# A last product's last K pair by column halves, and two swapped load buffers

## The chip, the cores and the metric

The kernel runs on one core of a Trainium2 chip. The metric is the device time of one execution in microseconds (us). TensorE (PE in the profile) multiplies; VectorE (DVE), ScalarE (ACT) and GpSimd (POOL) work on tiles; SyncE (SP) issues most DMAs. Matrix products are summed in PSUM, which the other engines read from; everything else is held in SBUF.

## What is computed

One Conformer-like encoder layer on 256 tokens of width 2048, in float32: two half-weighted SwiGLU feed-forwards with 5632 hidden features, between them a mixing layer and a cross-attention into 256 memory tokens, and a final RMS norm. What matters here is the end:

```python
def swiglu_ffn(h, w_in, w_out):
    gate, up = jnp.split(h @ w_in, 2, axis=-1)
    return (jax.nn.silu(gate) * up) @ w_out
...
    h = rms_norm(x, ffn2_norm[l])
    x = x + MACARON_SCALE * swiglu_ffn(h, ffn2_w_in[l], ffn2_w_out[l])
return rms_norm(x, final_norm)
```

## The kernel before

**Products in two parts.** Every float32 operand is split into a rounded part and its remainder (`hi` and `lo`; ACT rounds, DVE subtracts), and a product is three matmuls: hi by hi, hi by lo, lo by hi. The split weights lie in tiles `hl`, of which there are a few in turn.

**The second feed-forward, first product.** `FeedForward.run` goes through the 5632 hidden features in eleven groups j of 512 (gate and up together 1024 columns), and within a group through 16 K tiles k of 128 features. Some pairs of K tiles are done in a form with seven products in place of eight (`seven`), the others plainly (`eight`). For a few plain tiles the split isn't made by DVE: the raw tile is loaded, ACT writes the rounded part and the negated raw tile (L426, L427), and POOL issues a DMA that loads the weights a second time and adds them onto the negated copy (L428). These are the "summed" tiles. In the second feed-forward (`pair=True`) they are K tiles 2, 7 and 13 of groups 1 to 7 and K tiles 2 and 10 of groups 8 to 10, 27 in all, listed in order in `sums_at`. The code of such a tile is `summed`.

They live in two buffers for the split tile, `hls[0]` (a tile of its own, `hl_s`) and `hls[1]` (`hl_s2`), with a raw buffer each: `raws_summed[0]` is a part of `spare`, `raws_summed[1]` is the place of hidden group 8, `h8`. From group 8 on the second pair is given up: group 8's result is written to `h8`, and `hl_s2`'s place is taken by groups 9 and 10. `buffer(at)` (L411) says which buffer an entry of the list has; `following(at)` finds the next entry with the same buffer. When `eight` has issued the matmuls of a summed tile, it notes the following entry, and that entry's load and copies are issued behind the next cast of the ordinary stream. Entry 0 is issued in group 0 at K tile 13, entry 1 behind group 0.

**The last product.** The hidden features are turned (transposed through TensorE) into tiles `hA`, `hB`, `hC`, and multiplied by `ffn2_w_out` in four blocks of 512 output columns. For the fourth block (L1276 and below) the two blocks of 128 tokens are set apart, so that the first can be finished while the second is multiplied: the 44 K tiles go in 22 pairs; all pairs are multiplied for token block 0 in order, and for token block 1 too, but for the last four pairs, whose split weights are kept (the first of these four in a tile `held`) and multiplied for block 1 at the end. `acc[0]` and `acc[1]` are one PSUM bank each (128 partitions by 512 columns). `by_token` issues the six matmuls of a pair.

**The end of a token block.** `add_up` adds half the product onto the residual `x2` (DVE, L1227), squares it with a running sum into a column of `sums` (ACT, L1231), and multiplies by the final gain (POOL, L1232). The sums of the first three blocks are gathered earlier into `most`, one value a token. `give` takes the root of the whole sum (L1238 to L1242), scales the row and stores it, in 2 parts for token block 0 and in 4 for block 1; the last part is scaled by ACT (L1248), the others by DVE (L1251).

**Order.** The order of each engine's instructions is made by a planner, which takes those whose operands are ready by its own reckoning and prefers what is written first; `tc.issue_after` holds it to an order in some places. Semaphores between engines are put in by the same tool. Small tiles of the pool `st` lie ahead of most larger pools; two fillers of 32 bytes, `to_64` and `to_64_too`, are among them.

Of the kernel before, what the change touches and what calls it, by code (L numbers as in the profile page):

```python
# [11 lines left out]
F32 = mybir.dt.float32  # L12
F32R = mybir.dt.float32r
AF = mybir.ActivationFunctionType
ALU = mybir.AluOpType
AX = mybir.AxisListType

P = 128
D = 2048
# [59 lines left out]
def layer(ctx: ExitStack, tc: tile.TileContext, a: dict):  # L79
    nc = tc.nc  # L80
    out = a["out"]
# [6 lines left out]
    st = ctx.enter_context(tc.tile_pool(name="st", bufs=1))  # L88
# [85 lines left out]
    def gemm_t(w, x_hl, per=0.0, acc=None, ks=None, joint=False, between=None):  # L174

        return ahead([w], x_hl, per, [acc], ks, joint, between=between)[0]
# [59 lines left out]
    def col(name, k):  # L236
        return pv[:, PV[name][0] + k:PV[name][0] + k + 1]
# [104 lines left out]
    class FeedForward:  # L342
# [67 lines left out]

        def buffer(self, at):  # L411

            return at % 2 if not self.pair or self.sums_at[at][0] < 8 else 0

        def following(self, at):
            same = [i for i in range(at + 1, len(self.sums_at)) if self.buffer(i) == self.buffer(at)]
# [384 lines left out]
    with ExitStack() as stack:  # L801
        with tc.tile_pool(name="mix", bufs=1) as pool:
# [78 lines left out]
            for n in range(NCT // 2):  # L881
                if n < 2:
                    acc = gemm_n(a["w_mix_vg"][n], lambda k: x_hl[:, k], per=1.35, between=turns, acc=accs[n], ks=range(8, KD, 2))
                else:
                    load_gate(n)
                    later.appendleft((1.6, memory_parts(n)))
                    acc = gemm_n(a["w_mix_vg"][n], lambda k: x_hl[:, k], per=1.35, between=turns, after=2)
# [3 lines left out]
                for t in range(2):  # L891
# [3 lines left out]
                        out=o[:, t], in0=acc[t][:, :T], scalar=r_t[:, t:t + 1], in1=tg, op0=ALU.mult, op1=ALU.mult  # L895
# [48 lines left out]
            for n in range(2):  # L944
                acc = gemm_n(a["w_mix_v"][n], lambda k: x_hl[:, k], per=1.35, between=turns)
                for t in range(2):
                    nc.scalar.activation(
                        out=vs[:, t, n * 512:(n + 1) * 512], in_=acc[t], func=AF.Gelu, scale=r_t[:, t:t + 1]
# [60 lines left out]
            for n in range(HEADS):  # L1009
                acc = gemm_n(a["w_k"][n], lambda k: m_hl[:, k], per=1.35, between=turns)  # L1010
# [16 lines left out]
            for n in range(2):  # L1027
                acc = gemm_n(a["w_mix_u"][n], lambda k: x_hl[:, k], per=1.35, between=turns)
# [13 lines left out]
            at = [part for _, part in later].index(conv_swish_0)  # L1042
# [10 lines left out]
            for h in range(HEADS):  # L1053
                acc = gemm_n(a["w_v"][h], lambda k: m_hl[:, k], per=1.6)
                for t in range(2):
                    nc.scalar.activation(
                        out=vv[:, t, h * HD:(h + 1) * HD], in_=acc[t], func=AF.Copy, scale=r_mt[:, t:t + 1]
# [8 lines left out]
            for f in range(KD):  # L1066
                if f < 3:
                    acc = gemm_t(a["w_mix_out"][f], lambda k: y_hl[:, k], acc=accs[f], ks=[(0, 8)])
                else:
                    acc = gemm_t(a["w_mix_out"][f], lambda k: y_hl[:, k])  # L1070
# [3 lines left out]
        with tc.tile_pool(name="attn", bufs=1) as pool:  # L1074
# [112 lines left out]
            for f in range(KD):  # L1187
                if f < 4:
                    acc = gemm_t(a["w_o"][f], o_of, acc=accs[f], ks=[(12, 4)] if f < 3 else [(8, 8)])
                else:  # L1190
                    acc = gemm_t(a["w_o"][f], o_of)
# [3 lines left out]
    with ExitStack() as stack:  # L1195
        ff = FeedForward(stack, ("S0", "S1", "S2"), x_hl, lambda k: col("ffn2_norm", k), a["ffn2_w_in"], PATTERNS[1], SUMMED[1], pair=True)
        x2 = ff.x2

        def turn(n, i, j):

            def go():
                q = j % 4
                dst = x2[32 * q:32 * q + 32, j // 4, n * 512:(n + 1) * 512].rearrange("p (f n) -> p f n", n=P)
                nc.vector.transpose(
                    out=dst[:, :, 32 * i:32 * i + 32],
                    in_=xT[32 * i:32 * i + 32, 4 * n:4 * n + 4, 32 * j:32 * j + 32],
                )
            return go

        h = ff.of  # L1210
        def first_beside(k):
            if k in (6, 9, 12):
                ff.sides(k // 3 - 2)

        turns = ff.run(lambda k: None, first_beside, lambda: rms_cols(ss, D, "r_x2"))
        put(0.3, *[turn(0, i, j) for i in range(4) for j in range(8)])
        acc_0 = gemm_n(a["ffn2_w_out"][0], h, per=0.55, between=turns, after=0)
        finish()
        ff.high.close()
        stack.enter_context(ff.late)  # L1220
        late = stack.enter_context(tc.tile_pool(name="late", bufs=1, reuse_waits="tile"))
        gf = late.tile([P, D], F32, name="gf")
        nc.sync.dma_start(out=gf, in_=a["final_norm"].partition_broadcast(P))
        sums = st.tile([P, 2, 4], F32, name="sums")

        def add_up(t, s, acc, i):
            nc.vector.scalar_tensor_tensor(  # L1227
                out=x2[:, t, s], in0=acc, scalar=0.5, in1=x2[:, t, s], op0=ALU.mult, op1=ALU.add
            )
            sq = late.tile([P, 512], F32, name="sq2")  # L1230
            nc.scalar.activation(out=sq, in_=x2[:, t, s], func=AF.Square, accum_out=sums[:, t, i:i + 1])  # L1231
            nc.gpsimd.tensor_tensor(out=x2[:, t, s], in0=x2[:, t, s], in1=gf[:, s], op=ALU.mult)  # L1232

        def give(t, parts):

            v, s, r = [st.tile([P, 1], F32, name=f"{n}{t}") for n in ("f_v", "f_s", "f_r")]
            last = sums[:, t, 3:4]
            nc.scalar.activation(out=s, in_=last, func=AF.Sqrt, scale=1.0 / D, bias=most[t])  # L1238
            nc.vector.tensor_scalar(out=v, in0=last, scalar1=1.0 / D, scalar2=most[t], op0=ALU.mult, op1=ALU.add)
            nc.vector.reciprocal(out=r, in_=s)  # L1240
            nc.vector.tensor_scalar(out=r, in0=v, scalar1=r, scalar2=s, op0=ALU.mult, op1=ALU.add)
            nc.vector.reciprocal(out=r, in_=r)  # L1242
            for i, (at, size) in enumerate(cuts(D, D // parts)):
                c = slice(at, at + size)
                if i == parts - 1:
                    r2 = st.tile([P, 1], F32, name=f"f_r2{t}")
                    nc.scalar.mul(out=r2, in_=r, mul=2.0)
                    nc.scalar.activation(out=x2[:, t, c], in_=x2[:, t, c], func=AF.Copy, scale=r2)  # L1248
                    nc.scalar.dma_start(out=out[t * P:(t + 1) * P, c], in_=x2[:, t, c])
                else:  # L1250
                    nc.vector.tensor_scalar(  # L1251
                        out=x2[:, t, c], in0=x2[:, t, c], scalar1=r, scalar2=2.0, op0=ALU.mult, op1=ALU.mult
                    )
                    nc.sync.dma_start(out=out[t * P:(t + 1) * P, c], in_=x2[:, t, c])

        for n in range(3):
            if n == 1:
                put(0.3, *[turn(m, i, j) for m in range(1, 4) for i in range(4) for j in range(8)])
            acc = gemm_n(a["ffn2_w_out"][n], h, per=0.75) if n else acc_0
            for t in range(2):  # L1260
                add_up(t, slice(n * 512, (n + 1) * 512), acc[t], n)
        finish()


        st.tile([P, 8], F32, name="to_64_too")
        most = [st.tile([P, 1], F32, name=f"f_most{t}") for t in range(2)]
        for t in range(2):
            nc.vector.reduce_sum(out=most[t], in_=sums[:, t, 0:3], axis=AX.X)
            nc.vector.tensor_scalar(
                out=most[t], in0=most[t], scalar1=1.0 / D, scalar2=RMS_EPS, op0=ALU.mult, op1=ALU.add  # L1270
            )


        warm = nc.scalar.activation(out=st.tile([P, 1], F32, name="warm"), in_=ones[:, 0:1], func=AF.Sqrt)
        tc.keep_in_program_order(warm)
        w = a["ffn2_w_out"][3]  # L1276
        acc = [ps.tile([P, 2, 256], F32, name="acc").rearrange("p a b -> p (a b)") for _ in range(2)]
        parts = cuts(KF, 2)
        held = late.tile([P, 2, 1024], F32R, name="held")
        kept = []  # L1280

        def by_token(t, k0, hi, lo):
            for k in range(2):
                x = h(k0 + k)[:, :, t * P:(t + 1) * P]
                first, last = k0 + k == 0, k0 + k == KF - 1
                nc.tensor.matmul(acc[t], lhsT=x[:, 0], rhs=hi[:, k], start=first, stop=False)
                nc.tensor.matmul(acc[t], lhsT=x[:, 0], rhs=lo[:, k], start=False, stop=False)
                nc.tensor.matmul(acc[t], lhsT=x[:, 1], rhs=hi[:, k], start=False, stop=last)

        for i, (k0, kk) in enumerate(parts):  # L1290
            left = len(parts) - i
            hi, lo = weights(w[:, k0:k0 + kk, :], kk, 512, held if left == 4 else None)
            by_token(0, k0, hi, lo)
            if left > 4:
                by_token(1, k0, hi, lo)
            else:
                kept.append((k0, hi, lo))
        add_up(0, slice(1536, 2048), acc[0], 3)
        give(0, 2)
        for k0, hi, lo in kept:  # L1300
            by_token(1, k0, hi, lo)
        add_up(1, slice(1536, 2048), acc[1], 3)
        give(1, 4)


# [64 lines left out]
```

## Time and profile before

| | us |
|---|---|
| median of 3 runs (lowest, highest) | 2088.95 (2088.29, 2089.90) |
| the profiled execution's own time | 2088.91 |
| its span, first to last instruction | 2087.1 |
| TensorE busy | 2076.4 |
| VectorE busy | 1622.5 |
| ScalarE busy | 1174.4 |
| GpSimd busy | 66.0 |

The mean granted TensorE clock was 0.999 of full speed. A row of the timeline gives the start in us from the span's start, the duration, the engine, the line of the kernel, the operation, the tile written and the tiles read, the shape and a count; in brackets stands how long the engine had been idle before it and what ended that. A row of waits gives the waiting and the releasing instruction, the total, the number of times and the longest. A row of instructions by line gives the least, median and largest duration in ns.

### The profile page before, as it was taken

What the parts mean: (1) busy time and instruction counts of PE and PEld (TensorE: products, weight loads), DVE (VectorE), ACT (ScalarE), POOL (GpSimd) and SP (SyncE); (2) the same over time, 40 slices, a digit from 0 to 9 for tenths busy, and PEclk for the clock granted to TensorE, in tenths of its full rate; (3) what the DMA queues carried; (4) which work ended last, traced back from release to release, by engine and by line L of the source; (5) the groups of instructions that cost most, each with busy time, mean ns of one, the idle gap of its engine ahead of it and who ended that gap; (6) DMA issues with size and microseconds to landing.
All of it is one profiled execution on the core that took longest, in us unless ns stands there. A gap on an engine that the chain in (4) does not pass through costs nothing.

```text
span 2087.1 us, 26730 instructions
## 1 busy us (share of the span) xinstructions
PE 2076.4 (99%) x9765; PEld 1739.0 (83%) x9765; DVE 1622.5 (78%) x2302; ACT 1174.4 (56%) x1470; POOL 66.0 (3%) x81
## 2 busy tenths in 40 slices
PE   9999999999999999999999999999999999999998
PEld 8888888888888888888888899888888888888886
DVE  7888888877777689989877666778888888787754
ACT  8665666555545554445764455566665655554443
POOL 0000000000000000000000000000000000000000
PEclk9999999999999999999999999999999999999999
DMA  9787778755566576655555543687777777556664
GB/s 366 246 263 246 232 223 263 230 182 192 188 203 234 180 238 199 186 179 187 180 196 192 184 160 124 200 291 224 237 236 253 222 217 230 169 166 203 195 192 152
DMA packets 122245, 441.30 MB, mean 211 GB/s; under 512 B 13569, under 2 KB 13953, under 8 KB 121729
## 3 DMA queue, kind: packets, MB, share of 16 engines
q1 hardware_dynamic: 113184, 407.08, 57.1%
q0 software_dynamic: 8352, 31.46, 8.1%
q8 instruction: 76, 1.25, 0.2%
q10 hardware_dynamic: 576, 1.06, 0.1%
q14 instruction: 57, 0.46, 0.1%
HBM read 437.44 MB, written 2.10 MB: 211 GB/s over the span
## 4 chain that ended last, share of the span: by engine, by line
PE 87%; issue 11%; POOL 1%; DMA 1%; ACT 0%; DVE 0%; DVEq 0%; POOLq 0%
PE acc L332 11%; PE acc L331 11%; PE acc L334 11%; PE acc L204 8%; PE acc L205 8%; PE acc L203 8%; PE acc L154 8%; PE acc L162 4%; PE acc L318 3%; PE acc L319 3%; PE acc L320 3%; PE aux L306 1%; PE aux L318 1%; PE aux L319 1%; PE aux L320 1%
## 5 line engine op out<-in xcount | busy, mean ns | idle before, releaser
L124 ACT CAST hl<-raw 128x1024 fp32r<-128x1024 f32 (+1 forms) x315 | 327.1, 1040 | 358.9 <-PE acc L205 191.9
L125 DVE TENSOR_TENSOR hl<-raw,hl 128x1024 fp32r<-128x1024 f32 (+1 forms) x315 | 381.2, 1212 | 165.0 <-ACT hl L124 163.6
L397 ACT CAST hl<-raw 128x1024 fp32r<-128x1024 f32 (+1 forms) x151 | 147.6, 988 | 117.3 <-PE acc L334 48.2
L398 DVE TENSOR_TENSOR hl<-raw,hl 128x1024 fp32r<-128x1024 f32 (+1 forms) x151 | 172.2, 1145 | 47.4 <-ACT hl L397 45.7
L398 DVE TENSOR_TENSOR hl<-spare,hl 128x1024 fp32r<-128x1024 f32 (+1 forms) x125 | 144.7, 1162 | 32.5 <-ACT hl L397 30.3
L397 ACT CAST hl<-spare 128x1024 fp32r<-128x1024 f32 (+1 forms) x125 | 124.3, 1002 | 66.4 <-PE acc L334 24.2
L332 PE MATMUL acc<-hl,x_hl 128*128 128x512 f32 x388 | 140.9, 390 | 0.1
L331 PE MATMUL acc<-hl,x_hl 128*128 128x512 f32 x388 | 135.7, 390 | 0.0
L334 PE MATMUL acc<-hl,x_hl 128*128 128x512 f32 x388 | 120.6, 390 | 0.0
L397 ACT CAST ring<-spare 128x1024 fp32r<-128x1024 f32 (+1 forms) x83 | 82.1, 993 | 59.6 <-issue 19.1
L398 DVE TENSOR_TENSOR ring<-spare,ring 128x1024 fp32r<-128x1024 f32 (+1 forms) x83 | 95.2, 1150 | 20.3 <-ACT ring L397 19.6
L332 PE MATMUL acc<-ring,x_hl 128*128 128x512 f32 x276 | 101.3, 389 | 0.0
L204 PE MATMUL acc<-hl,x_hl 128*128 128x512 f32 x256 | 100.7, 393 | 0.0
L204 PE MATMUL acc<-hl,m_hl 128*128 128x512 f32 x256 | 100.4, 392 | 0.0
L205 PE MATMUL acc<-hl,m_hl 128*128 128x512 f32 x256 | 100.3, 392 | 0.0
L205 PE MATMUL acc<-hl,x_hl 128*128 128x512 f32 x256 | 100.0, 391 | 0.0
L331 PE MATMUL acc<-ring,x_hl 128*128 128x512 f32 x276 | 98.6, 390 | 0.0
L203 PE MATMUL acc<-hl,m_hl 128*128 128x512 f32 x256 | 90.9, 392 | 0.0
L203 PE MATMUL acc<-hl,x_hl 128*128 128x512 f32 x256 | 90.2, 392 | 0.0
L334 PE MATMUL acc<-ring,x_hl 128*128 128x512 f32 x276 | 86.2, 389 | 0.0
L332 PEld LDWEIGHTS acc<-hl,x_hl 128*128 128x128 f32 x388 | 72.6, 188 | 15.5 <-DVE hl L133 0.4
L334 PEld LDWEIGHTS acc<-hl,x_hl 128*128 128x128 f32 x388 | 72.9, 188 | 15.1
(518 smaller groups left out, 5100.8 us busy)
## 6 DMA issues: line engine op xcount, KB each, us to landing
spare<-in_ffn_w_in SPq DMA_DIRECT2D x184, 512.0 KB, 6.8
raw<-in_ffn_w_in SPq DMA_DIRECT2D x157, 512.0 KB, 5.9
raw<-in_ffn_w_out SPq DMA_DIRECT2D x138, 512.0 KB, 4.0
hl_s<-in_ffn_w_in POOLq DMA_DIRECT2D x42, 512.0 KB, 8.3
raw<-in_w_mix_vg SPq DMA_DIRECT2D x32, 512.0 KB, 4.3
raw<-in_w_k SPq DMA_DIRECT2D x32, 512.0 KB, 3.6
raw<-in_w_v SPq DMA_DIRECT2D x32, 512.0 KB, 4.0
raw<-in_w_mix_out SPq DMA_DIRECT2D x32, 512.0 KB, 4.4
```

What stands on the lines that cost most here:

```text
L124: nc.scalar.copy(out=hl[:, 0, :size], in_=raw[:, :size])
L125: newest[0] = nc.vector.tensor_tensor(out=hl[:, 1, :size], in0=raw[:, :size], in1=hl[:, 0, :size].bitcast(F32), op=ALU.subtract)
L154: done = nc.tensor.matmul(acc, lhsT=hi[:, k], rhs=xs[k], start=first and k == 0, stop=last and k == kk - 1, skip_group_check=True,)
L162: done = nc.tensor.matmul(acc[:, 0], lhsT=lo[:, k], rhs=xs[k][:, 0], start=False, stop=last and k == kk - 1, skip_group_check=True,)
L203: nc.tensor.matmul(acc[t], lhsT=x[:, 0, s], rhs=hi[:, k], start=k0 + k == 0, stop=False)
L204: nc.tensor.matmul(acc[t], lhsT=x[:, 0, s], rhs=lo[:, k], start=False, stop=False)
L205: nc.tensor.matmul(acc[t], lhsT=x[:, 1, s], rhs=hi[:, k], start=False, stop=k0 + k == nk - 1)
L331: nc.tensor.matmul(acc[t][g], lhsT=x[:, 0, s], rhs=hi[:, cols[g]], start=(t, g) in first, stop=False)
L332: nc.tensor.matmul(acc[t][g], lhsT=x[:, 0, s], rhs=lo[:, cols[g]], start=False, stop=False)
L334: nc.tensor.matmul(acc[t][g], lhsT=x[:, 1, s], rhs=hi[:, cols[g]], start=False, stop=last)
L397: self.cast = nc.scalar.copy(out=hl[:, 0, :n], in_=raw[:, :n])
L398: newest[0] = nc.vector.tensor_tensor(out=hl[:, 1, :n], in0=raw[:, :n], in1=hl[:, 0, :n].bitcast(F32), op=ALU.subtract)
```

## The change

The buffers of the summed tiles in the second feed-forward are swapped for groups below 8. In the last product the last of the four kept pairs is multiplied for token block 1 first into columns 0 to 255 of `acc[1]`, all six products of it, and then into columns 256 to 511; behind each half its 256 columns are added up. The square sum of the first half is added onto `most` by a new small instruction, `add_most`, and `sums` has a fifth column. Token block 0 uses columns 0 to 2 and 4 of it.

```diff
         def buffer(self, at):
-            return at % 2 if not self.pair or self.sums_at[at][0] < 8 else 0
+            if self.pair:
+                return (at + 1) % 2 if self.sums_at[at][0] < 8 else 0
+            return at % 2
...
-        sums = st.tile([P, 2, 4], F32, name="sums")
+        sums = st.tile([P, 2, 5], F32, name="sums")
...
-            sq = late.tile([P, 512], F32, name="sq2")
+            sq = late.tile([P, 512], F32, name="sq2")[:, :acc.shape[-1]]
...
-            last = sums[:, t, 3:4]
+            last = sums[:, t, 4:5]
...
+        def add_most(t, i):
+            nc.vector.scalar_tensor_tensor(
+                out=most[t], in0=sums[:, t, i:i + 1], scalar=1.0 / D, in1=most[t], op0=ALU.mult, op1=ALU.add
+            )
...
-        def by_token(t, k0, hi, lo):
+        def by_token(t, k0, hi, lo, c=slice(0, 512)):
...
-                nc.tensor.matmul(acc[t], lhsT=x[:, 0], rhs=hi[:, k], start=first, stop=False)
+                nc.tensor.matmul(acc[t][:, c], lhsT=x[:, 0], rhs=hi[:, k, c], start=first, stop=False, skip_group_check=True)
...
-        add_up(0, slice(1536, 2048), acc[0], 3)
+        add_up(0, slice(1536, 2048), acc[0], 4)
         give(0, 2)
-        for k0, hi, lo in kept:
+        for k0, hi, lo in kept[:-1]:
             by_token(1, k0, hi, lo)
-        add_up(1, slice(1536, 2048), acc[1], 3)
+
+        for i in range(2):
+            by_token(1, *kept[-1], slice(i * 256, (i + 1) * 256))
+            add_up(1, slice(1536 + i * 256, 1792 + i * 256), acc[1][:, i * 256:(i + 1) * 256], 3 + i)
+            if i == 0:
+                add_most(1, 3)
         give(1, 4)
```

More of the change, by code (lines that the diff above doesn't have):

```diff
@@ L1285, in by_token @@
                 first, last = k0 + k == 0, k0 + k == KF - 1
-                nc.tensor.matmul(acc[t], lhsT=x[:, 0], rhs=hi[:, k], start=first, stop=False)
-                nc.tensor.matmul(acc[t], lhsT=x[:, 0], rhs=lo[:, k], start=False, stop=False)
-                nc.tensor.matmul(acc[t], lhsT=x[:, 1], rhs=hi[:, k], start=False, stop=last)
+                nc.tensor.matmul(acc[t][:, c], lhsT=x[:, 0], rhs=hi[:, k, c], start=first, stop=False, skip_group_check=True)
+                nc.tensor.matmul(acc[t][:, c], lhsT=x[:, 0], rhs=lo[:, k, c], start=False, stop=False, skip_group_check=True)
+                nc.tensor.matmul(acc[t][:, c], lhsT=x[:, 1], rhs=hi[:, k, c], start=False, stop=last, skip_group_check=True)
         for i, (k0, kk) in enumerate(parts):
```

## Prediction

> **What bounds the kernel now.** I read the page's first part, then TensorE's waits, then the timeline in the two places that the change touches: hidden group 8 of the second feed-forward and the last fifteen microseconds.
>
> ```profile
> PE 2076.4 (99%) x9765; PEld 1739.0 (83%) x9765; DVE 1622.5 (78%) x2302; ACT 1174.4 (56%) x1470; POOL 66.0 (3%) x81
> PE aux L232 <- DVE ones L229: 1.1, 1, 1.1
> PE acc L332 <- DMA hl_s<-in_ffn_w_in: 0.8, 1, 0.8
> ```
>
> TensorE is busy for 2076.4 of 2087.1 us, and its whole list of waits has two entries. Of 10.7 us without a matmul, 1.1 lie before the first one, 0.8 in one wait for a load into `hl_s`, and most of the rest behind the last matmul. So only three things can move the time: TensorE's own work, that wait, and the tail behind the last matmul. The change touches the second and the third, and the first a little.
>
> **The swapped buffers.** The wait lies here:
>
> ```profile
> 1705.95 0.39 PE L331 MATMUL acc<-hl_s,x_hl 128*128 128x512 f32 x1
> 1707.13 0.50 PE L332 MATMUL acc<-hl_s,x_hl 128*128 128x512 f32 x1 [0.80 <-DMA hl_s<-in_ffn_w_in]
> 1707.47 0.39 PE L334 MATMUL acc<-hl_s,x_hl 128*128 128x512 f32 x1
> 1707.70 0.40 PE L318 MATMUL acc<-hl,ring 128*128 128x512 f32 x1
> ```
>
> POOL's issues around it, and the time that a load of `hl_s` takes to land:
>
> ```profile
> 1669.77 0.86 POOL L428 DMA_DIRECT2D hl_s<-in_ffn_w_in  x1 [12.05 <-ACT hl_s L426]
> 1698.32 0.86 POOL L428 DMA_DIRECT2D hl_s<-in_ffn_w_in  x1 [27.69 <-ACT hl_s L426]
> 1712.34 0.89 POOL L428 DMA_DIRECT2D hl_s<-in_ffn_w_in  x1 [13.15 <-ACT hl_s L426]
> ...
> DMA to landing us min/median/max: 5.2/8.3/9.8
> ```
>
> Starts of neighbouring matmuls are 0.23 apart (1707.47 to 1707.70). Here they are 1.18 and 0.34 apart, so the wait costs 0.95 + 0.11, about 1.07 us with its slow restart. Its cause stands in POOL's rows: the adding load for tile (8, 2), group 8 and K tile 2, goes out at 1698.32, after a pause of 27.69 where other pauses are 12 to 15; with 8.3 us to land it comes at about 1706.6.
>
> The code says why. The list of summed tiles is (1,2), (1,7), (1,13), (2,2) and so on to (7,13), which is entry 20, then (8,2) as entry 21. A buffer's next load is issued when its last tile has been multiplied. By `at % 2`, entry 20 has buffer 0, and from group 8 on all entries have buffer 0. So (8,2) follows (7,13), the tile just before it, and after (7,7) nothing is loaded. With `(at + 1) % 2`, (7,7) has buffer 0 and (8,2) follows it; (7,13) has buffer 1 and nothing follows. The same number of loads goes out; one moves forward by one place.
>
> ```profile
> 1679.20 0.39 PE L331 MATMUL acc<-hl_s,x_hl 128*128 128x512 f32 x1
> 1683.07 1.05 ACT L397 CAST hl<-spare 128x1024 fp32r<-128x1024 f32 x1 [2.58 <-PE aux L320]
> ...
> 1640.19 1.06 ACT L426 ACTIVATE hl_s<-spare 128x1024 fp32r<-128x1024 f32 x1 [1.17 <-PE acc L332]
> 1641.16 1.03 ACT L427 CAST hl_s<-spare 128x1024 fp32r<-128x1024 f32 x1
> 1642.10 1.05 ACT L397 CAST hl<-raw 128x1024 fp32r<-128x1024 f32 x1
> ```
>
> (7,7) is multiplied by twelve matmuls 0.23 apart, from 1679.20 to about 1682.1. ACT then makes the two copies for (8,2), some 2.0 us, and POOL issues near 1684.2, so the data lands at 1692.5, or 1694.0 by the longest landing: 12 us before its use. The SP load of the raw tile moves with it, into a buffer that (7,7)'s copies freed long before. What is moved past: ACT's ordinary cast at 1683.07, which had 2.58 idle before it and now starts about a microsecond later. The cover for that is shown one group earlier, where the same two copies stand ahead of the same cast (1640.19 to 1642.10) and TensorE's list has no wait. If that cover failed, it would cost at most the two copies' 2.0 us less the slack of the split tiles ahead. At the start of the stage the first two entries merely exchange buffers; TensorE waits for neither now, and I cost that at nothing. **Gain: 1.07 us**, bounded by 0 (the load doesn't come forward) and 1.1.
>
> **The last pair by halves.** Six matmuls of 512 columns become twelve of 256, with twelve weight loads. The price of a 256-column matmul with a fresh weight load stands in the output products:
>
> ```profile
> 1302.27 3.04 PE L162 MATMUL acc<-o_hl,hl 128*128 128x256 f32 x24
> L294 DVE SCALAR_TENSOR_TENSOR xT<-acc,xT x64: 414/425/426, 1086.9 to 1369.5; 128x256 f32<-128x256 f32 x64
> L257 ACT ACTIVATE sq<-xT x45: 399/402/419, 652.4 to 1371.4; 128x256 f32<-128x256 f32 x45
> ```
>
> (3.04 - 0.28) / 23 = 0.120 a start, 0.28 being the duration of one. Six take 0.72 where half of the six wide ones took 0.68: twelve cost TensorE 0.08 more. An addition of 256 columns out of PSUM takes 0.425 in place of 0.68, a square 0.40 in place of 0.63 (the wide ones stand in the next rows).
>
> ```profile
> 2070.26 0.39 PE L1286 MATMUL acc<-held,hC 128*128 128x512 f32 x1
> ...
> 2076.83 0.39 PE L1286 MATMUL acc<-hl,hC 128*128 128x512 f32 x1
> 2077.96 0.39 PE L1288 MATMUL acc<-hl,hC 128*128 128x512 f32 x1
> ...
> 2077.76 0.17 DVE L1242 RECIPROCAL f_r<-f_r 128x1 f32<-128x1 f32 x1
> 2078.03 0.78 DVE L1251 TENSOR_SCALAR spare<-spare,f_r 128x1024 f32<-128x1024 f32 x1
> 2078.74 0.68 DVE L1227 SCALAR_TENSOR_TENSOR spare<-acc,spare 128x512 f32<-128x512 f32 x1
> ...
> 2078.30 1.15 ACT L1248 ACTIVATE spare<-spare,f_r 128x1024 f32<-128x1024 f32 x1
> 2079.45 0.63 ACT L1231 ACTIVATE sq<-spare 128x512 f32<-128x512 f32 x1
> 2079.98 0.19 ACT L1231 ACTIVATION_READ_ACCUMULATOR sq<-spare 128x1 f32 x1
> 2080.20 0.21 DVE L1239 TENSOR_SCALAR f_v<-sums,f_most 128x1 f32<-128x1 f32 x1 [0.79 <-ACT sq L1231]
> 2080.25 1.26 POOL L1232 TENSOR_TENSOR spare<-spare,gf 128x512 f32<-128x512 f32 x1 [1.98 <-ACT sq L1231]
> 2081.23 1.35 DVE L1251 TENSOR_SCALAR spare<-spare,f_r 128x512 f32<-128x512 f32 x3
> 2081.54 0.72 ACT L1248 ACTIVATE spare<-spare,f_r 128x512 f32<-128x512 f32 x1
> ```
>
> The reader should see that token block 1's add and square aren't late by TensorE alone. The last matmul ends at 2078.35, but the add starts at 2078.74, behind token block 0's scaling (L1251), and the square at 2079.45, the moment that ACT is done with its share of that scaling (L1248, 1.15 us). From the sum at 2080.17 a fixed chain leads to 2081.23, three scalings to 2082.58, and the last store.
>
> In the new order, in the old trace's times: the first half starts at 2076.83, its last matmul starts at 2077.43 and ends at 2077.71. DVE adds it behind L1242, from 2077.95 to 2078.37. No row shows DVE reading one half of a PSUM bank while TensorE writes the other, so I bound this both ways. If the second half waits for the add, it starts at 2078.40, its last start is 2079.00, its end 2079.28 plus 0.11 of restart, and the second add runs from 2079.42 to 2079.85; nothing but those six matmuls stands behind that wait on TensorE. If it doesn't wait, it ends at 2078.43, and the second add can end at 2078.88. ACT decides between the two: it has L1248 until 2079.45, then two squares. One of 512 takes 0.72 with its read-out (2079.45 to 2080.17), one of 256 then 0.72 - 0.23 = 0.49, so they end at 2079.94 and 2080.43. The new small addition (`add_most`, like L1239 0.21) fits between 2079.94 and 2080.43. So the sum is there 0.26 us later than now. POOL's halves end before the scaling asks for them if half the columns take about half of 1.26; if each took all of it, ACT's last scaling would end near 2083.2 and the tail be 0.6 later. **Cost: 0.26 us**; bounds: a gain of 0.8, if both squares got ahead of L1248 and the second half didn't wait (2078.88 + 0.49 = 2079.37 for the sum), and a loss of 1.05, which the first rival works out.
>
> The Trainium skill, PSUM — Partial Sum Buffer, section "PSUM bank collisions raise a hardware error", says that any two engines on one bank and quadrant at once raise an error even at disjoint columns, so they have to be ordered by bank. No run here shows it yet. By that rule the waiting case holds; the forecast's 0.26 is the same by either, but without it the first rival below would cost 0.26 too.
>
> **Sum**, against the profiled execution's own 2088.91 us (span 2087.1): 2088.91 - 1.07 + 0.26 = 2088.10. The median of the runs shown, 2088.95, lies 0.04 above that execution, so the forecast for the median is 2088.1. About 0.2% (4.2 us) is what a measurement of this kernel can tell from no change; the forecast is well within it.
>
> **The rivals.**
>
> *The add is queued behind the scaling.* In the program's text `give(0)` stands ahead of the new adds. If DVE has L1251 first, the first add runs from 2078.81 to 2079.24; with the bank's wait, the second half ends at 2080.26, its add at 2080.72, its square at 2081.22: the tail is 1.05 later and the total 2088.91 - 1.07 + 1.05 = 2088.89. For it: the text's order. Against it: the first half is done at 2077.71, 0.32 before L1251 starts, and the planner already goes by readiness: a matmul on `held`, written behind `give(0)`, stands at 2070.26 among token block 0's.
>
> *The swap does nothing.* The load of (8,2) comes forward, but something else is late by as much: 2088.91 + 0.26 = 2089.17. For it: ACT is given 2.0 us in a group that ends in close-set casts. Against it: group 6 does just that without a wait.
>
> *Slower: everything behind the small tiles moves by 32 bytes.* `sums` grows from 32 to 40 bytes; by the kernel's 32-byte fillers `to_64` and `to_64_too`, 40 bytes take two places, and all later pools (`hl_s` among them) would start 32 bytes off a multiple of 64. If loads to such places took longer, the single buffer of groups 8 to 10 would pay first:
>
> ```profile
> 1776.30 0.86 POOL L428 DMA_DIRECT2D hl_s<-in_ffn_w_in  x1 [21.62 <-ACT hl_s L426]
> 1790.00 0.39 PE L331 MATMUL acc<-hl_s,x_hl 128*128 128x512 f32 x1
> 1728.35 0.39 PE L331 MATMUL acc<-hl_s,x_hl 128*128 128x512 f32 x1
> ```
>
> From issue to use (10,2) has 13.7 us and (8,10), issued at 1712.34, has 16.0; the longest landing is 9.8, so it decides from loads that take 40% longer. At twice the median, 16.6, the five tiles would be late by 0.6 to 2.9, some 9 us in all: 2097. For it: the fillers exist. Against it: I find no row in which the place of a tile shows in a duration.
>
> **How the numbers follow.** The forecast 0.58, the add behind the scaling 0.22, the swap without effect 0.07, the shift by 32 bytes 0.07; 0.03 each for an unnamed loss and gain of over 4 us. The first three are within 0.2%: 0.87 same, 0.10 slower, 0.03 faster. The range takes the bounds, 2088.91 - 1.07 - 0.8 = 2087.0 and 2088.91 + 1.05 = 2090.0, and some of the scatter of the runs (2088.29 to 2089.90): 2086.8 to 2090.4.
>
> **What would show it.** TensorE's waits lose the row on `hl_s`; POOL's issue for (8,2) stands near 1684; the last pair shows two groups of six 256-column matmuls 0.12 apart, with about 1.0 from the last start of the one to the first of the other if the bank makes them wait, and 1.8 if the add is behind L1251 too; ACT goes from L1248 straight into two squares. A new wait of TensorE on a load anywhere, or landings well over 9.8, would prove the sum wrong.

## The result, and the profile after

| | before | after |
|---|---|---|
| median, us (lowest to highest, runs) | 2089.28 (2088.29 to 2089.90, 6) | 2099.94 (2099.77 to 2100.08, 6) |
| ratio, 95% interval | | 1.0051 (1.0040 to 1.0062) |
| span of the profiled execution, us | 2087.1 | 2098.2 |
| mean granted TensorE clock | 0.999 | 0.999 |

The kernel is 0.5% slower, 10.7 us, where 2088.1 was forecast and 2090.4 was the end of the range. First part of the page of the kernel after, and the row of its DMA issues for `hl_s` (the last number is the median from issue to landing):

```profile
span 2098.2 us, 26747 instructions
...
PE 2088.3 (100%) x9771; PEld 1739.2 (83%) x9771; DVE 1623.1 (77%) x2304; ACT 1176.0 (56%) x1472; POOL 66.5 (3%) x82
...
hl_s<-in_ffn_w_in POOLq DMA_DIRECT2D x42, 512.0 KB, 8.5
```

TensorE was busy for 2076.4 us and is now busy for 2088.3, with six more matmuls: its busy time grew by 11.9 and the span by 11.1. The granted clock is the same. All of TensorE's waits after (waiting and releasing instruction, total, times, longest):

```profile
PE aux L232 <- DVE ones L229: 1.1, 1, 1.1
PE acc L1293 <- DVE spare L1229: 0.5, 1, 0.5
```

The wait on `hl_s` is gone, and the only new one, 0.5 us, is the second half of the last pair waiting for the add. So no wait explains the loss: the matmuls themselves stand further apart. The windows of TensorE show where. Columns: the stretch, its length, busy time and number of matmuls, granted clock, DMA share, GB/s. Before:

```profile
55.00:440.00 385.00, 385.00 (x1700) 1.00 0.76 239
...
1830.00:2050.00 220.00, 220.00 (x1009) 1.00 0.60 190
```

and after:

```profile
55.00:440.00 385.00, 385.00 (x1675) 1.00 0.76 236
...
1830.00:2050.00 220.00, 220.00 (x1007) 1.00 0.58 186
```

In the first feed-forward, which the diff doesn't touch, TensorE is busy all the time in both, at the same clock, and gets through 25 matmuls fewer in 385 us: 25 times 0.227 is 5.7 us, half of the loss, before 440 us. (In the later windows the two programs stand at different places, so their counts compare less well. Compared by the n-th matmul of the program, the kernel after is 5.9 us late at 415 us, 8.2 at 740 and still 8.1 at 1377, 9.15 at 1641, 8.4 at 1710 behind the removed wait, and 10.7 where the last pair starts.)

Which matmuls? Rows by line and tiles: least, median and largest duration in ns, first and last start. Before:

```profile
L331 PE MATMUL acc<-more,x_hl x96: 388/389/390, 67.5 to 432.0; 128*128 128x512 f32 x96
L203 PE MATMUL acc<-hl,hC x48: 388/390/398, 1886.8 to 2017.7; 128*128 128x512 f32 x48
L331 PE MATMUL acc<-hl,x_hl x388: 388/389/486, 5.4 to 1828.1; 128*128 128x512 f32 x194
```

After:

```profile
L331 PE MATMUL acc<-more,x_hl x96: 392/394/399, 68.4 to 438.3; 128*128 128x512 f32 x96
L203 PE MATMUL acc<-hl,hC x48: 392/395/396, 1895.9 to 2027.9; 128*128 128x512 f32 x48
L331 PE MATMUL acc<-hl,x_hl x388: 387/389/774, 5.8 to 1837.2; 128*128 128x512 f32 x194
```

By the medians, the same instruction on the same line keeps its 389 ns where it reads `hl` and `x_hl`, and ends 5 to 6 ns later where it reads `more`, `hl_s` or `hC`. The starts show it too. Timeline of TensorE, four neighbouring matmuls, before and after:

```profile
67.53 0.39 PE L331 MATMUL acc<-more,x_hl 128*128 128x512 f32 x1
67.75 0.39 PE L332 MATMUL acc<-more,x_hl 128*128 128x512 f32 x1
67.98 0.39 PE L331 MATMUL acc<-more,x_hl 128*128 128x512 f32 x1
68.21 0.39 PE L332 MATMUL acc<-more,x_hl 128*128 128x512 f32 x1
```

```profile
68.42 0.40 PE L331 MATMUL acc<-more,x_hl 128*128 128x512 f32 x1
68.65 0.39 PE L332 MATMUL acc<-more,x_hl 128*128 128x512 f32 x1
68.88 0.40 PE L331 MATMUL acc<-more,x_hl 128*128 128x512 f32 x1
69.12 0.40 PE L332 MATMUL acc<-more,x_hl 128*128 128x512 f32 x1
```

(68.21 - 67.53) / 3 = 0.227 and (69.12 - 68.42) / 3 = 0.233. Over all 333 matmuls of `more` by `x_hl` the mean from start to start rose from 226.7 to 233.4 ns, for `hl_s` by `x_hl` in the first feed-forward from 226.7 to 233.5, for `hl` by `hC` at the end from 228.3 to 234.1.

What the slower ones have in common is their place in SBUF, as the two programs lay it out (bytes from a partition's start):

```
               before   after
x_hl, ring       3584    3584    (more of them at 36352 and 69120)
hl             118272  118272    (and 126464, 134656)
sums, size         32      40
more           158208  158240
hl_s           175104  175136
hC             183296  183328
hl_s2          216576  216576
```

`sums` grew from 32 to 40 bytes, takes two 32-byte places in place of one, and everything allocated behind the pool of small tiles stands 32 bytes further on. What lies ahead of that pool, and `hl_s2`, which is placed from the other end, doesn't move. Some 1,320 matmuls of 512 columns have one operand in a tile that moved and the other in one that didn't; by 6 to 7 ns each that is 8 to 9 us.

The two places that the change aimed at, after. POOL's issues around hidden group 8 (timeline; idle time and releaser in brackets):

```profile
1679.03 0.87 POOL L430 DMA_DIRECT2D hl_s<-in_ffn_w_in  x1 [12.10 <-ACT hl_s L428]
1692.47 0.87 POOL L430 DMA_DIRECT2D hl_s<-in_ffn_w_in  x1 [12.57 <-ACT hl_s L428]
1720.73 0.89 POOL L430 DMA_DIRECT2D hl_s<-in_ffn_w_in  x1 [27.39 <-ACT hl_s L428]
```

The pause of 27 us stands one issue later: the load of (8, 2) goes out at 1692.47, 13.4 us behind the issue ahead of it, where it was 28.6 (1669.77 to 1698.32). The last pair (timeline of TensorE, DVE and ACT):

```profile
2087.53 0.28 PE L1293 MATMUL acc<-hl,hC 128*128 128x256 f32 x1
...
2088.11 0.28 PE L1295 MATMUL acc<-hl,hC 128*128 128x256 f32 x1
2088.43 0.42 DVE L1229 SCALAR_TENSOR_TENSOR spare<-acc,spare 128x256 f32<-128x256 f32 x1
2088.77 0.15 DVE L1244 RECIPROCAL f_r<-f_r 128x1 f32<-128x1 f32 x1
2088.89 0.42 ACT L1233 ACTIVATE sq<-spare 128x256 f32<-128x256 f32 x1 [1.01 <-DVE spare L1229]
...
2088.91 0.39 PE L1293 MATMUL acc<-hl,hC 128*128 128x256 f32 x1 [0.52 <-DVE spare L1229]
2089.03 0.75 DVE L1253 TENSOR_SCALAR spare<-spare,f_r 128x1024 f32<-128x1024 f32 x1
...
2089.30 0.19 ACT L1249 ACTIVATE f_r<-f_r 128x1 f32<-128x1 f32 x1
...
2089.58 1.15 ACT L1250 ACTIVATE spare<-spare,f_r 128x1024 f32<-128x1024 f32 x1
...
2089.70 0.69 DVE L1276 SCALAR_TENSOR_TENSOR f_most<-sums,f_most 128x1 f32<-128x1 f32 x1
...
2090.31 0.41 DVE L1229 SCALAR_TENSOR_TENSOR spare<-acc,spare 128x256 f32<-128x256 f32 x1
2090.76 0.42 ACT L1233 ACTIVATE sq<-spare 128x256 f32<-128x256 f32 x1
2091.08 0.19 ACT L1233 ACTIVATION_READ_ACCUMULATOR sq<-spare 128x1 f32 x1
```

Two groups of six, 0.116 a start, with 0.80 from the last start of the first group to the first of the second. The second square starts 0.03 behind L1250, ACT's share of token block 0's scaling. The sum stands at 2091.27, 3.74 us behind the start of the last pair, where it was 3.34 (2076.83 to 2080.17): 0.40 later. From that start to the end of the span it is 10.65 in place of 10.31: 0.34 later.

### The profile page after: what moved, and what is told of

It is laid out like the page before. It is cut to its first block, busy times and chain, and to the rows that moved or that the text cites. A ratio compares the mean times of both kernels' runs of the same rounds, so it can differ in the third digit from the quotient of the medians.

```text
span 2098.2 us, 26747 instructions
## 1 busy us (share of the span) xinstructions
PE 2088.3 (100%) x9771; PEld 1739.2 (83%) x9771; DVE 1623.1 (77%) x2304; ACT 1176.0 (56%) x1472; POOL 66.5 (3%) x82
## 4 chain that ended last, share of the span: by engine, by line
PE 99%; DVE 0%; ACT 0%; DVEq 0%; issue 0%
PE acc L332 13%; PE acc L331 13%; PE acc L334 13%; PE acc L204 8%; PE acc L205 8%; PE acc L203 8%; PE acc L154 8%; PE acc L162 4%; PE acc L318 4%; PE acc L319 4%; PE acc L320 4%; PE aux L318 1%; PE aux L319 1%; PE aux L320 1%; PE aux L306 1%; PE acc L1294 1%
## 5 line engine op out<-in xcount | busy, mean ns | idle before, releaser
L397 ACT CAST hl<-spare 128x1024 fp32r<-128x1024 f32 (+1 forms) x125 | 124.6, 1003 | 67.8 <-PE acc L334 28.6
L332 PE MATMUL acc<-hl,x_hl 128*128 128x512 f32 x388 | 140.9, 391 | 0.0
L331 PE MATMUL acc<-hl,x_hl 128*128 128x512 f32 x388 | 135.9, 392 | 0.0
L332 PE MATMUL acc<-ring,x_hl 128*128 128x512 f32 x276 | 101.4, 390 | 0.0
L331 PE MATMUL acc<-ring,x_hl 128*128 128x512 f32 x276 | 98.8, 390 | 0.0
L331 PEld LDWEIGHTS acc<-hl,x_hl 128*128 128x128 f32 x388 | 72.9, 188 | 15.6
L332 PEld LDWEIGHTS acc<-hl,x_hl 128*128 128x128 f32 x388 | 72.7, 188 | 15.7 <-DVE hl L398 0.3
```

The lines of the kernel that those rows point to most:

```text
L331: nc.tensor.matmul(acc[t][g], lhsT=x[:, 0, s], rhs=hi[:, cols[g]], start=(t, g) in first, stop=False)
L332: nc.tensor.matmul(acc[t][g], lhsT=x[:, 0, s], rhs=lo[:, cols[g]], start=False, stop=False)
L397: self.cast = nc.scalar.copy(out=hl[:, 0, :n], in_=raw[:, :n])
```

## The experiments

Each kernel is given by its difference from the kernel before or, where the text says so, from the changed one. The theory was that the place of the tiles costs some 11 us, while the swap gains about 1 and the halves cost a few tenths. Rivals: the swap or the halves cost it themselves, or the size of `sums` does it in another way than by place. All times are medians, beside the kernel before on the same chip.

| run | us | before, us | ratio (95%) |
|---|---|---|---|
| e1_change_in_place | 2088.50 | 2089.58 | 0.9995 (0.9987 to 1.0004) |
| e2_before_32 | 2101.10 | 2089.58 | 1.0056 (1.0043 to 1.0068) |
| e3_before_64 | 2100.54 | 2089.58 | 1.0052 (1.0039 to 1.0064) |
| e4_swap_alone | 2088.14 | 2089.58 | 0.9992 (0.9983 to 1.0001) |
| e5_halves_alone | 2090.03 | 2089.52 | 1.0000 (0.9992 to 1.0009) |
| e6_before_128 | 2098.86 | 2089.52 | 1.0043 (1.0027 to 1.0058) |
| e7_before_256 | 2089.72 | 2089.52 | 1.0001 (0.9992 to 1.0010) |
| e8_before_512 | 2089.79 | 2089.52 | 1.0000 (0.9991 to 1.0009) |
| e9_all_64 | 2089.93 | 2089.70 | 1.0000 (0.9991 to 1.0010) |
| e10_xt_32 | 2100.43 | 2089.70 | 1.0052 (1.0035 to 1.0069) |
| e11_swap_ident | 2087.54 | 2089.67 | 0.9991 (0.9982 to 0.9999) |
| e12_swap_again | 2088.25 | 2089.67 | 0.9993 (0.9984 to 1.0002) |

**The whole change, with no tile moved.** The change as it is, but without the filler of 32 bytes, so that the larger `sums` takes its place:

```diff
-        st.tile([P, 8], F32, name="to_64_too")
```

> The whole change, but without the filler of 32 bytes (to_64_too), so that sums' 40 bytes move nothing behind it. Place theory (matmuls that read a tile 32 bytes off a multiple of 64 start 6 to 7 ns further apart): the 11.8 us go, 1.07 of the removed wait stay as a gain and 0.36 of the tail as a loss, 2089.3 - 1.07 + 0.36 = 2088.6. Order theory (the swap or the halves made TensorE's stream slower): 2099.9 as with the change.

2088.50, 1.1 us below before. The window of TensorE in the first feed-forward has its 1700 matmuls again:

```profile
55.00:440.00 385.00, 385.00 (x1700) 1.00 0.77 239
```

and the rows by line have their durations:

```profile
L331 PE MATMUL acc<-more,x_hl x96: 389/389/389, 68.0 to 432.4; 128*128 128x512 f32 x96
L203 PE MATMUL acc<-hl,hC x48: 389/389/398, 1886.1 to 2017.0; 128*128 128x512 f32 x48
```

The computation changed and the tiles didn't, and the loss is gone.

**The kernel before, with its tiles moved.** No instruction differs from the kernel before; one more filler stands among the small tiles, of 32 or 64 bytes:

```diff
         st.tile([P, 8], F32, name="to_64_too")
+        st.tile([P, 8], F32, name="to_32_more")
```

> The kernel before with one more filler of 32 bytes behind to_64_too: the same moves of all later pools as in the change, nothing else. Place theory: 2089.3 + 11.8 = 2101.1, with 233 ns from start to start for matmuls on more and hl_s in the first feed-forward, where it was 227. Order theory: 2089.3. Landing theory (the moved loads take longer): waits of TensorE on loads; the place theory has none but the 0.8 of before.

> The kernel before with 64 bytes more in the same place. If what counts is the distance to a multiple of 64: 2089.3, no change. If what counts is any move off the old places (they were multiples of 512 for more and hl_s): about 2101.

2101.10 and 2100.54: an unused tile alone costs 11.5 and 11.0 us. So the place is the cause, and it isn't a matter of multiples of 64, which the names of the fillers suggest: there the theory missed, and its measure was still to be found. Rows by line of the kernel moved by 32:

```profile
L331 PE MATMUL acc<-more,x_hl x96: 392/394/399, 68.2 to 438.0; 128*128 128x512 f32 x96
L203 PE MATMUL acc<-hl,hC x48: 392/395/396, 1897.0 to 2029.0; 128*128 128x512 f32 x48
```

They are the rows of the kernel after, with its starts to within about 1 us.

**The swap alone, and the halves alone.** The first is the diff of `buffer`; the second is all the rest, with the filler taken out as in the first run.

> The kernel before with the two buffers swapped and nothing else; no tile moves. Place theory: TensorE's wait on hl_s is gone and nothing takes its place, 2089.3 - 1.07 = 2088.2. Order theory: the swap carries some or all of the loss, up to 2100.

> The swap alone once more beside it: 1.1 to 1.4 us below the kernel before.

> The last pair by halves with sums of 40 bytes, the swap undone, and without the filler of 32 bytes, so that no tile moves. Place theory: only the tail is longer, by the 0.36 read in the changed kernel's trace: 2089.6 + 0.4 = 2090.0. If the halves save what they were written for, below 2089.6.

The swap alone gives 2088.14, and 2088.25 in a second series: 1.44 and 1.42 us below before. POOL's timeline with the swap alone:

```profile
1670.16 0.87 POOL L430 DMA_DIRECT2D hl_s<-in_ffn_w_in  x1 [12.04 <-ACT hl_s L428]
1683.82 0.87 POOL L430 DMA_DIRECT2D hl_s<-in_ffn_w_in  x1 [12.80 <-ACT hl_s L428]
1711.64 0.89 POOL L430 DMA_DIRECT2D hl_s<-in_ffn_w_in  x1 [26.95 <-ACT hl_s L428]
```

The issue for (8, 2) stands at 1683.82, and of TensorE's two waits of before only the one at the start, on `ones`, is left. The halves alone give 2090.03, 0.5 us above before; both differences are small, and the intervals hold 1. The traces tell more. Compared by the n-th matmul of the program, the kernel with the swap alone is 0.39 us later than the kernel before at the start of the removed wait and 0.70 earlier at its end, a gain of 1.09; the second series shows the same gain (0.30 later, 0.79 earlier). From the start of the last pair to the end of the span it is 10.66 with the halves alone and 10.66 with the whole change in place, and 10.30 to 10.32 before and with the swap alone in both series: a loss of 0.35. The wait on `hl_s`, still in the kernel with the halves alone, varies beside that: 1.3 in its trace, 0.8 before.

**How far counts.** The same filler with 128, 256 and 512 bytes:

> The kernel before with 128 bytes more behind the small tiles. 32 and 64 bytes each cost 11 to 12 us. If the step is 128: 2089.6. If it is longer (256, 512, or one place is special): 2100 to 2101.

> The same with 256 bytes. Step of 256 or less: 2089.6. Step of 512, or the old place as such: about 2100.

> The same with 512 bytes, so that hl_s, more and hC are at multiples of 512 again. Step of 512 or less: 2089.6. If the old places as such matter (or how far the tiles are from others), about 2100.

By 128 bytes it costs 9.3 us, by 256 and 512 nothing. The row of `more` by line, moved by 128 and then by 256:

```profile
L331 PE MATMUL acc<-more,x_hl x96: 387/398/404, 67.9 to 436.4; 128*128 128x512 f32 x96
```

```profile
L331 PE MATMUL acc<-more,x_hl x96: 389/389/389, 68.0 to 432.5; 128*128 128x512 f32 x96
```

**A tile's own place, or its place against the other operand's?** 64 bytes ahead of all pools, and 64 less in the filler of the pool that is placed from the other end, so that every tile that a product reads moves by 64:

```diff
+    const.tile([P, 16], F32, name="all_64")
     ones = const.tile([P, P], F32, name="ones")
...
-                high.tile([P, 120], F32, name="to_512")
+                high.tile([P, 104], F32, name="to_512")
```

> The kernel before with 64 bytes ahead of all other tiles (and 64 fewer in the filler to_512 of the second feed-forward), so that all tiles that TensorE reads move by 64 together. If the place of a tile by itself counts, nearly every 512-column matmul starts some 3 to 7 ns further apart: over 7000 of them, 2089.6 + 20 to 50 us. If the place of the one operand against the other counts (weights and columns, or the tiles of neighbouring matmuls), they stand as before: about 2089.6.

2089.93 beside 2089.70: nothing, where 64 bytes under a part of the tiles cost 11.0. The row by line (the kernel is one line longer, so that it names L332 for what was L331):

```profile
L332 PE MATMUL acc<-more,x_hl x96: 389/389/389, 67.7 to 432.2; 128*128 128x512 f32 x96
```

So no tile has to lie at a multiple of anything. What counts is how the tile that is read as columns lies against the one that is read as weights: at the same place modulo 256 bytes, as near as these sizes tell, nothing is lost.

Which two reads that is stays open: a matmul's own columns and weights, or its columns and the weights of the next one, whose load starts together with them. Two rows of the kernel before, TensorE's matmul and the load of the next matmul's weights (LDWEIGHTS):

```profile
2077.51 0.39 PE L1286 MATMUL acc<-hl,hC 128*128 128x512 f32 x1
2077.51 0.19 PEld L1287 LDWEIGHTS acc<-hl,hC 128*128 128x128 f32 x1
```

Nearly all these matmuls stand in rows that read the same two tiles, so both are off together. At the ten places where moved weights begin behind unmoved ones, the step from the last unmoved matmul to the first moved one grew from 227 ns to about 235 with 32 bytes and 233 with 128, which speaks for the weights of the next; with 64 it stayed at 227, which doesn't.

**Two different offsets.** A filler of 32 bytes ahead of `more`'s place and one behind it, so that `more` is 32 off and the tiles behind it 64:

```diff
+    xt.tile([P, 8], F32, name="ahead")
     gx = xt.tile([P, P + KD * T], F32, name="gx", tag="x")
...
     gains, xT = gx[:, P - KD:P], gx[:, P:].rearrange("p (k t) -> p k t", t=T)
+    xt.tile([P, 8], F32, name="behind")
```

> The kernel before with 32 bytes ahead of the pool that holds more, and 32 behind it: more is 32 off its place and all later tiles are 64 off theirs. If 32 and 64 are equally bad, as the two whole moves say, it costs what they cost, 2100 to 2101; the matmuls on more start 233 ns apart as in the kernel moved by 32, those on hl_s as in the one moved by 64.

2100.43, 10.7 above before: below all by 32 (11.5) and all by 64 (11.0), by less than the scatter, so the time doesn't tell the shares of the tiles apart. The starts do, as expected. The 333 matmuls of `more` by `x_hl` stand 233.3 ns apart, as with all moved by 32 (233.4; by 64 it is 230.5); those of `hl_s` by `x_hl` in the first feed-forward stand 231.1 apart, as with all moved by 64 (231.1; by 32 it is 233.5). Each follows the offset of its own tile.

**Does it hold for the transposes?** In the kernel before one pair of operands is off: `ident` stands at 1664, 128 bytes past a multiple of 256, and most tiles that it transposes stand at one. With the swap, and 128 bytes ahead of and behind `ident`, it stands at a multiple of 256 and everything behind it moves by 256:

```diff
+    const.tile([P, 32], F32, name="ahead")
     ident = const.tile([P, P], F32, name="ident")
+    const.tile([P, 32], F32, name="behind")
```

> The swap alone, and the identity tile of the transposes moved by 128 bytes, to a multiple of 256 like the tiles that are transposed against it (all later tiles move by 256, which cost nothing above). If the relative place counts for the 128-column float32 transposes too: 256 of them, each up to 3 ns closer, 0 to 0.8 us below the swap alone's 2088.1, with starts under 108 ns apart. If not: 2088.1 and 108 ns.

The rows of the transposes, by line, with `ident` moved and with the swap alone:

```profile
L308 PE MATMUL aux<-ident,h x160: 270/272/275, 448.0 to 1877.1; 128*128 128x128 f32 x160
```

```profile
L306 PE MATMUL aux<-ident,h x160: 270/272/273, 448.3 to 1877.7; 128*128 128x128 f32 x160
```

They take 272 ns in both, and neighbouring ones stand 108.6 ns apart in both: the transposes, 128 columns of plain float32, show no such cost at 128 bytes, and the theory's expectation for them missed. The kernel is 0.7 us faster than the swap alone (2087.54 beside 2088.25): the time fell within the range that the theory gave, but not by its way. Of the 0.6 us between the two profiled executions 0.2 is there by 10 us, where executions of one program differ by as much; 0.1 comes between 440 and 900 us, and 0.2 between 1822 and 1900, where transposes stand between the last products. What it comes from stays open. It is the fastest version measured, 2.1 us below before.

## Why the prediction was wrong

**Its two terms held; a third was left at nothing.** With no tile moved the change takes 1.1 us off (2089.58 to 2088.50), where the sum -1.07 + 0.26 said 0.81; in the traces the two terms are 1.09 and 0.35. Moving the tiles alone adds 11.5 (e2). Put together, 11.5 - 1.4 for the swap + 0.5 for the halves = 10.6, and the whole change measured 10.7.

**The step that failed** is the first one: "So only three things can move the time: TensorE's own work, that wait, and the tail behind the last matmul. The change touches the second and the third, and the first a little." The little was the twelve half matmuls of the last pair, 0.08 us. The change touched the first in some 1,320 matmuls, through the size of one small tile. In a kernel whose TensorE is busy for 2076.4 of 2087.1 us, 6 ns on a seventh of 9,765 matmuls outweigh every wait that is left.

**The rival on the slower side had the right event and the wrong mechanism.** It said that `sums` would take two places and that all later tiles would move by 32 bytes, and priced that by slower loads: five late tiles, 9 us. The loads landed as before (8.5 us against 8.3 in the median, 9.8 at the longest in both), and TensorE has no new wait on one. The price came out near by chance: it was paid by the matmuls that read the moved tiles. The sentence "I find no row in which the place of a tile shows in a duration" was true of that trace, since there the operands of all the 512-column products stood alike modulo 256; what doesn't vary in a trace can't show its price. That speaks for a wide bound, and the rival was given 0.07 and left outside of the range instead.

**The swap** did as forecast: the row on `hl_s` is gone, the issue was forecast "near 1684" and stands at 1683.82 with the swap alone, and ACT's cast a microsecond later cost nothing. Across the wait it gained 1.09 in the trace, where the sum had 1.07; the medians say 1.4.

**The halves** went by the waiting case, with two differences. The second half did wait for the add: 0.52 us idle, 0.80 between the starts where 0.97 was worked out. This agrees with the rule in the Trainium skill, PSUM — Partial Sum Buffer, section "PSUM bank collisions raise a hardware error", that two engines must not be on one bank and quadrant at once even at disjoint columns: the program orders them, and no run here shows what happens without the order. And the add did get ahead of L1253, the scaling that was L1251. But it got in ahead of L1244 too, one link of token block 0's own chain, which the forecast had as finished. That link starts 1.24 behind the start of the last pair (2088.77 - 2087.53) where it started 0.93 behind it. Then ACT's first square, at 2088.89, gets ahead of ACT's own link (L1249, at 2089.30). Together they put off ACT's scaling: it starts 2.05 us behind the start of the last pair (2089.58 - 2087.53) where it started 1.47 behind it (2078.30 - 2076.83). The second square follows the scaling at once. The sum came 0.40 later where 0.26 was forecast, so the direction was right. That ACT decides is not shown. `add_most` (L1276) stands ahead of the second add on DVE and takes 0.69 us, where the forecast had 0.21 and gave it no place ahead of that add; the add ends at 2090.72 and ACT's scaling at 2090.73, and the profile's chain of work that ended last runs through the first.

**How sure.** That the place is the cause is shown in both directions, by e1 and e2. That the relative place of columns and weights counts is shown by e9 against e3, and tile by tile by e10; whether it is the weights of the same matmul or of the next isn't shown. That it counts modulo 256, by e6 against e7 and e8; offsets that aren't multiples of 32 weren't tried. Why the pair costs time is not shown. The direct part, some 1,330 matmuls by 6 to 7 ns, is 8 to 9 of 11.5 us. The rest shows on matmuls beside them: in the first feed-forward `hl` by `x_hl`, with no moved operand, went from 227.4 to 229.1 ns a start. They are the ones right behind. Set start by start against the kernel before, which has the same instructions, the kernel moved by 32 bytes loses 8.6 us on the matmuls of 512 columns with one moved operand, 2.9 on the seven or fewer that follow each row of them, and 0.2 on all others. How a loss is carried on to matmuls whose operands stand alike is open as well.

## What to carry to other kernels

Where TensorE is the bound, take a change in the size of any tile as seriously as a change in the work: lay out the addresses before and after, and ask which matmuls now read two operands that no longer stand alike modulo 256 bytes. A filler that brings the tiles behind it back to where they were repairs it (here, taking 32 bytes out of one, worth 11 us). When a trace has TensorE busy throughout and no new wait, compare the number of matmuls in a stretch that the change doesn't touch: 1700 against 1675 told in one row what no list of waits could.

## What the hardware showed that was not expected

A float32 product matmul of 128 by 512 with weights of its own started 226.7 ns behind the one before it when its weights and its columns lay alike modulo 256 bytes, and about 233 ns when one of the two lay 32 bytes off, whichever of them it was: in the rows above `more` is read as columns and `hC` as weights. Offsets of 32, 64 and 128 bytes cost 11.5, 11.0 and 9.3 us in all, 256 and 512 none, and 64 under every tile none. The Trainium skill, TensorE: Matmul & The Clock Gate, section "Step-by-step: what each phase is for", gives the weights and the columns a read port each, independent of one another; here the two reads don't look independent, as the pitch of the same instruction depends on where the one operand lies against the other.
